# Writing out TensorE's order for the up-projections in pairs in a decoder's second MLP

## The chip, the cores and the metric

The kernel runs on one core of one Trainium2 chip, which has eight. The metric is the device time of one execution in microseconds (us), the median over several runs. One more execution was profiled; all rows of the profile are from that one.

TensorE multiplies (PE in the profile; PEld is its loading of weights, which overlaps PE), VectorE (DVE) and ScalarE (ACT) work elementwise and can read TensorE's result banks, GpSimd (POOL) works elementwise on SBUF and issues the DMAs that accumulate, SyncE (SP) issues the other DMAs.

## The reference

The reference is a decoder trunk of two layers on 512 tokens of 1024 channels, in float32: a pooling mixer in the first layer, stick-breaking attention in the second, each between RMSNorms, and each followed by an MLP with 4096 hidden channels:

```
def sq_relu_mlp(h, w_up, w_down):
    u = jnp.matmul(h, w_up)                                  # (512, 1024) x (1024, 4096)
    return jnp.matmul(jnp.square(jax.nn.relu(u)), w_down)    # (512, 4096) x (4096, 1024)
...
    x = x + rms_norm(m, mix_post_g[layer])
    h = rms_norm(x, mlp_pre_g[layer])
    x = x + rms_norm(sq_relu_mlp(h, w_up[layer], w_down[layer]), mlp_post_g[layer])
```

Only the second of these MLPs is changed.

## The kernel before

**High and low parts.** A float32 operand is written as a high part, rounded by a copy to the type float32r, and a low part, operand minus high part. A product of two operands is three matmuls: high x high, high x low, low x high. So each matmul operand costs one pass of ScalarE (the high part) and one of VectorE (the low part), in `split`, L415 and L416. In `Pair.split` (L809) the low part of some operands is made without VectorE: ScalarE writes minus the high part (L812), and a DMA issued by POOL adds the source to it (L813). `BY_DMA` names these operands.

**The MLP.** The 4096 hidden channels are 32 blocks of 128. Groups of 2, 3, 3, 3 and 3 block pairs (`GROUPS`, 28 blocks) go through `Seven`, a 2x2 scheme of seven products instead of eight for the down-projection. One of its products (L727, "down product" below) is 2 banks x n pairs x 3 matmuls of 512 columns: 18 in a group of three. `make(i)` prepares the operands of product i, two products ahead: `right` combines pieces of the down weights by VectorE (L700), `left` combines quarters of the hidden activations r, in this MLP on POOL (L681), and both are split. The down weights of the next group are loaded by SyncE while a group ends (`coming.load`). The last four blocks go through `contract` at the end (L456 to L458).

**The up-projection.** While group g is multiplied down, the hidden blocks of group g + 1 are made. In a plain block (`up`, L1050 to L1052) a weight is loaded, split (L155, L157) and multiplied by the normed input, whose parts lie in `xnh` and `xnl`: 24 matmuls of 512 columns. In the second MLP the first `PAIRED` blocks are plain, and from there on two blocks each form a `Pair`, a 2x2 scheme again: seven products of 12 matmuls with 256 columns (L865 to L867). It needs:

- combinations t1 to t4 of quarters of the input, made once (`Sums`: L780, split at L783 and L784, a list of steps, one step per down product; t4 goes into a quarter of `xnh` and `xnl` that only the plain blocks need),
- combinations of the weights, for each pair: blocks A (`raw[0]`) and B (`raw[1]`, after L839 has put a difference into half of it), and S1, S2, S4 (L838, L842, L848).

`Pair.prepare(k)` is called when product k of the pair before has been issued, because the tile that it fills is the one that product k read: 1 prepares block A, s1 and the difference; 2 block B and s2; 6 splits S2; 5 splits S1 and makes s4; 3 splits S4; 0 loads the two raw weights (L807) of the pair after. Tiles are few: two raw tiles, one `spare` tile that holds s1 and s2, one `grow` tile for s4, three `w` tiles for A and B, one tile each for the parts of S1, S2 and S4. After a product, ScalarE (L873) or VectorE (L875) takes its bank out into r; products 1, 6, 5, 3 share one half of a bank, 7 and 4 the other. Then relu and square follow on ScalarE (L877 to L885).

**What sets the order.** Each engine works through its own queue in order. The order in these queues is settled when the program is built: a planner simulates the program with estimated costs and puts next on each engine what is ready then, earlier lines of the program first. `tc.manual_schedule(engines={...})` takes engines out of the planner's hands: what they do inside the block stands in the order in which the program names it. The attention is written so for all engines, the final contraction for TensorE. The groups of the MLP are planned. The two lines that name the order of a group of pair products, three pairs a, b, c, are:

```
"a1 a2 a7 a6,a4 a5 b1 b2,a3 b7 b6,b4 b5 c1,c2 b3 c7,c6 c4 c5,c3",
"a1 a2 a7,a6 a4 a5,a3 b1 b2,b7 b6 b4 b5,b3,,",
```

The parts between commas are the pair products that the program names after down products 0 to 6; the second line is for the last group, with two pairs. `ready(g, i)` works through one part. Before the change, pairs are multiplied in groups 1 to 4 (eleven pairs, for the blocks of groups 2 to 4 and the last four), and in group 0 the seven steps of `Sums` and the preparation of pair 0 run.

Of the kernel before, what the change touches and what calls it, by code (L numbers as in the profile page):

```python
# [15 lines left out]
P = 128  # L16
# [14 lines left out]
PAIRED = 10  # L31
BY_DMA = "A B S1 S4".split()
# [61 lines left out]
def trunk(ctx, tc, x, consts, gcol, grow, pw, wup, wdn, wq, wk, wv, wo, out):  # L94
# [646 lines left out]
    class Sums:  # L741
# [3 lines left out]
        def __init__(self):  # L745
# [11 lines left out]
            self.raw, self.whole = {}, whole  # L757
# [29 lines left out]
    class Pair:  # L787
# [40 lines left out]
        def prepare(self, behind):  # L828
            on = nc.vector.tensor_tensor
            if behind == 0:  # L830
                self.load()
                return
            (a11, a12), (a21, a22) = ([x[:, c] for c in NS] for x in self.raw)
            if behind == 1:
                self.block(0)
                both = spare_tile()
                self.s1, self.s2 = both[:, NS[0]], both[:, NS[1]]
                on(out=self.s1, in0=a21, in1=a22, op=ALU.add)  # L838
                on(out=a21, in0=a11, in1=a21, op=ALU.subtract)  # L839
            elif behind == 2:  # L840
                self.block(1)
                on(out=self.s2, in0=self.s1, in1=a11, op=ALU.subtract)  # L842
            elif behind == 6:
                self.third("S2", self.s2)
            elif behind == 5:
                self.third("S1", self.s1)
                self.s4 = work.tile([P, D], F32, tag="grow", name=name("s4"))[:, NS[0]]
                on(out=self.s4, in0=a12, in1=self.s2, op=ALU.subtract)  # L848
            elif behind == 3:
                self.third("S4", self.s4)  # L850
# [40 lines left out]
    def mlp(l, mp, update):  # L891
# [53 lines left out]
        if l == 1:  # L945
# [5 lines left out]
            for g in range(1, len(GROUPS)):  # L951
                for i, cell in enumerate(FIVE[g == len(GROUPS) - 1].split(",")):
                    plan[g, i] = []
                    for w in cell.split():
                        q = 3 * (g - 1) + "abc".index(w[0])
                        plan[g, i].append((q, int(w[1])))
            plan.update({(0, n): [(-1, int(x)) for x in w] for n, w in enumerate(("", "", "", "0", "12", "65", "3"))})

        def ready(g, i):
            if g == 0:  # L960
                sums.step()
            for q, which in plan[g, i]:
# [4 lines left out]
                if which == 5 and q + 2 < len(pairs):  # L967
                    pairs[q + 2].prepare(0)
# [21 lines left out]
        for g, group in enumerate(groups):  # L990
            coming = groups[g + 1] if g + 1 < len(groups) else None
            if coming:
                coming.squares()
            ups = list(range(firsts[g + 1], firsts[g + 1] + 2 * GROUPS[g + 1]) if coming else range(plain, NJ))
            if l == 1 and g > 0:
                ups = []
            if g == 0:
                up(ups.pop(0))
            for i in range(7):
                group.product(i, y, written if g == 0 else None)  # L1000
                if 7 * g + i in steps:
                    with tc.issue_after(latest["act"].ins), tc.issue_after(latest["dve"].ins):
                        split_apart(mp)
                if l == 1 and g > 0:
                    ready(g, i)
                    fill()
                if i + 2 < 7:
                    if ups:
                        up(ups.pop(0))
                    if l == 1 and g == 0:  # L1010
                        ready(g, i)
                    group.make(i + 2)
                    if i + 2 == 4 and coming:
                        coming.load(0)
                    if i + 2 >= 5 and coming:
                        coming.load(1, NS[1] if i + 2 == 5 else NS[0])
                else:
                    if ups:
                        up(ups.pop(0))
                    if l == 1 and g == 0:  # L1020
                        ready(g, i)
                    if coming:
                        coming.make(i + 2 - 7)
                    elif i == 5:
                        piece = lambda tag, k, bufs=1: mp.tile([P, k, D], F32R, tag=tag, bufs=bufs, name=name("dn"))
                        w, e, x = piece("w1", 3), piece("e", 1), piece("w", 3, 2)
                        if l == 0:
                            both = piece("apart", 3)
                            c, d = both[:, 0], both[:, 1]
                        else:  # L1030
                            c, d = (piece(f"part{n}", 1)[:, 0] for n in ("S1", "S2"))
                            for t in range(T):
                                xt[t] = work.tile([P, D], F32, tag=f"y{t}", name=name("x"))
                                nc.sync.dma_start(xt[t], saved[t])
                        dn_pool[0] = [[w[:, 0], w[:, 1]], [w[:, 2], e[:, 0]], [c, d], [x[:, 0], x[:, 1]]]
# [674 lines left out]
```

## Time and profile before

| | |
|---|---|
| median of 3 runs | 941.97 us (939.96 to 942.34) |
| the profiled execution's own time | 941.12 us |
| its span, first to last instruction | 939.3 us |
| mean granted TensorE clock | 0.972 |
| PE busy | 891.0 us |
| DVE, ACT, POOL busy | 728.2, 590.5, 122.0 us |
| second MLP's groups 0 to 4 | 590.8 to 906 us |

A row of a group of instructions gives line, engine, operation, output and inputs, shapes and count, then the busy time, the mean of one in ns, the idle time of the engine before them and what ended it. A row of a window gives its bounds, its length, the busy time and count of PE, PEld, DVE, ACT and POOL, the granted clock, the share of the DMA engines and GB/s. Matmuls overlap: what one costs is the step from its start to the next one's start. A few matmul records are missing from the trace, so counts are taken from the code.

### The profile page before, as it was taken

How to read it: one execution, taken by the hardware profiler on the slowest of the kernel's cores; microseconds unless marked ns; L12 is line 12 of the kernel's file. 1: busy time of each engine (PE TensorE's matmuls, PEld its weight loads, DVE VectorE, ACT ScalarE, POOL GpSimd, SP SyncE). 2: the span in 40 equal slices, each digit the busy share in tenths (PEclk: the TensorE clock that was granted, in tenths of full speed). 3: DMA queues.
4: the chain of work that ended last, by engine and by line, in shares of the span. 5: the costliest groups of instructions: out<-in, count | busy, mean ns of one | idle time of the engine just before them, and what ended most of it. 6: DMA issues, size and time to landing. Idle time of an engine off the chain costs nothing.

```text
span 939.3 us, 13155 instructions
## 1 busy us (share of the span) xinstructions
PE 891.0 (95%) x5024; PEld 785.7 (84%) x5024; DVE 728.2 (78%) x791; ACT 590.5 (63%) x1014; POOL 122.0 (13%) x127
## 2 busy tenths in 40 slices
PE   9999999999999999999999999997987897898896
PEld 7998888888888888888888889886977796797786
DVE  5865998989889766669999588859866677586856
ACT  6667666577888554458957254674665755856732
POOL 2100000000000041000000010425113301502303
PEclk9999999999999999999999999997998798999999
DMA  7444466387896408755565655365556574775532
GB/s 279 171 166 166 148 235 237 135 323 277 291 340 242 183 1 282 306 216 170 183 188 184 224 186 184 110 179 140 143 154 146 115 221 101 159 222 113 154 105 89
DMA packets 54885, 175.44 MB, mean 187 GB/s; under 512 B 5488, under 2 KB 9546, under 8 KB 54822
## 3 DMA queue, kind: packets, MB, share of 16 engines
q1 hardware_dynamic: 48338, 157.28, 47.7%
q0 software_dynamic: 6336, 17.30, 9.8%
q8 instruction: 39, 0.64, 0.3%
q14 instruction: 24, 0.20, 0.1%
q10 hardware_dynamic: 148, 0.02, 0.0%
HBM read 124.64 MB, written 32.64 MB: 167 GB/s over the span
## 4 chain that ended last, share of the span: by engine, by line
PE 74%; issue 7%; DVE 7%; DMA 7%; ACT 3%; POOL 2%; POOLq 0%; DVEq 0%; SPq 0%; ACTq 0%
PE ps L727 22%; PE ps L1050 9%; PE ps L1051 9%; PE ps L1052 9%; PE ps L1334 3%; PE ps L456 2%; PE ps L458 2%; PE ps L865 2%; PE ps L457 2%; DMA raw<-in_wup 2%; PE ps L867 2%; PE ps L866 2%; PE ps L1495 2%; PE ps L1410 2%; PE ps L1189 1%
## 5 line engine op out<-in xcount | busy, mean ns | idle before, releaser
L727 PE MATMUL ps<-w,a 128*128 128x512 f32 x1176 | 275.1, 385 | 8.7 <-ACT a L415 4.7
L727 PEld LDWEIGHTS ps<-w,a 128*128 128x128 f32 x1176 | 221.6, 192 | 41.8 <-ACT a L415 6.6
L1050 PE MATMUL ps<-xnh,w 128*128 128x512 f32 (+1 forms) x528 | 186.9, 356 | 0.0
L1051 PE MATMUL ps<-xnl,w 128*128 128x512 f32 (+1 forms) x528 | 186.6, 354 | 0.1
L1052 PE MATMUL ps<-xnh,w 128*128 128x512 f32 (+1 forms) x528 | 186.6, 354 | 0.0
L1052 PEld LDWEIGHTS ps<-xnh,w 128*128 128x128 f32 x528 | 100.2, 190 | 11.0 <-DVE w L157 0.2
L1051 PEld LDWEIGHTS ps<-xnl,w 128*128 128x128 f32 x528 | 100.2, 190 | 10.8 <-DVE xnl L416 0.3
L1050 PEld LDWEIGHTS ps<-xnh,w 128*128 128x128 f32 x528 | 99.5, 190 | 11.4 <-ACT xnh L415 0.4
L415 ACT CAST w<-e 128x1536 fp32r<-128x1536 f32 (+1 forms) x30 | 41.7, 1391 | 39.7 <-DVE e L700 24.4
L416 DVE TENSOR_TENSOR a<-r,a 128x768 fp32r<-128x768 f32 (+1 forms) x60 | 54.4, 907 | 8.3 <-ACT a L415 8.2
L416 DVE TENSOR_TENSOR w<-e,w 128x1536 fp32r<-128x1536 f32 (+1 forms) x30 | 49.9, 1662 | 13.5 <-ACT w L415 13.5
L1433 DVE TENSOR_TENSOR_SCAN e<-u,begin 128x1280 f32<-128x1280 f32 x16 | 44.9, 2808 | 13.4 <-ACT u L1424 13.3
L415 ACT CAST a<-r 128x768 fp32r<-128x768 f32 (+1 forms) x60 | 47.0, 784 | 12.3 <-POOL r L681 5.7
L739 DVE TENSOR_TENSOR x<-ps,x 128x512 f32<-128x512 f32 x62 | 41.6, 685 | 13.7 <-PE ps L727 13.6
L157 DVE TENSOR_TENSOR w<-raw,w 128x1024 fp32r<-128x1024 f32 x34 | 41.5, 1220 | 13.8 <-ACT w L155 13.8
L155 ACT CAST w<-raw 128x1024 fp32r<-128x1024 f32 x34 | 35.5, 1044 | 25.1 <-PE ps L1052 24.8
L739 DVE TENSOR_TENSOR y<-ps,y 128x512 f32<-128x512 f32 x62 | 41.7, 685 | 10.5 <-PE ps L727 10.4
L415 ACT CAST w<-xn 128x1536 fp32r<-128x1536 f32 (+1 forms) x20 | 27.8, 1389 | 30.5 <-PE ps L727 30.5
L810 ACT CAST w<-raw 128x1024 fp32r<-128x1024 f32 x22 | 23.0, 1045 | 35.9 <-DMA raw<-in_wup 24.4
L486 POOL TENSOR_TENSOR y<-y,grow 128x512 f32<-128x512 f32 x4 | 6.1, 1537 | 297.5 <-ACT xn L419 297.5
L865 PE MATMUL ps<-xnh,w 128*128 128x256 f32 x132 | 38.2, 292 | 5.4 <-ACT w L810 3.0
L432 POOL TENSOR_TENSOR stat<-stat,mhalf 128x1 f32<-128x1 f32 x20 | 12.0, 599 | 218.1 <-DVE stat L423 216.8
(262 smaller groups left out, 1975.2 us busy)
## 6 DMA issues: line engine op xcount, KB each, us to landing
raw<-in_wup SPq DMA_DIRECT2D x64, 512.0 KB, 3.6
w<-kept SPq DMA_DIRECT2D x42, 512.0 KB, 5.8
w<-in_wdn SPq DMA_DIRECT2D x8, 1536.0 KB, 7.0
xn<-in_wdn SPq DMA_DIRECT2D x16, 768.0 KB, 5.6
w<-raw POOLq DMA_DIRECT2D x22, 512.0 KB, 5.3
kept<-wx SPq DMA_DIRECT2D x20, 512.0 KB, 3.8
kept<-apart SPq DMA_DIRECT2D x16, 512.0 KB, 3.9
through<-turn SPq DMA_DIRECT2D x7, 896.0 KB, 3.5
```

What stands on the lines that cost most here:

```text
L155: nc.scalar.copy(hi, raw)
L157: nc.vector.tensor_tensor(out=lo, in0=raw, in1=hi.bitcast(F32), op=ALU.subtract)
L415: latest["act"] = nc.scalar.copy(hi, src)
L416: latest["dve"] = nc.vector.tensor_tensor(out=lo, in0=src, in1=hi.bitcast(F32), op=ALU.subtract)
L727: nc.tensor.matmul(bank, a[:, x, q, TS[t]], by_twos(w[:, z, q], NS[0]), start=start and q == 0 and k == 0, stop=q == self.n - 1 and k == 2 ...
L739: nc.vector.tensor_tensor(out=part, in0=bank, in1=part, op=ALU.add)
L865: nc.tensor.matmul(bank, wh[:, ws], xs[0], start=start and k == 0, stop=False, skip_group_check=True)
L1050: nc.tensor.matmul(pu[:, cols], wh[:, k, :], xh, start=k == 0, stop=False)
L1051: nc.tensor.matmul(pu[:, cols], wh[:, k, :], xl, start=False, stop=False)
L1052: nc.tensor.matmul(pu[:, cols], wl[:, k, :], xh, start=False, stop=k == KC - 1)
L1334: nc.tensor.matmul(bank, a[x][q], in_turn(w[q // 2][z][:, cols], 512), start=(i == 0 or not linked) and q == 0 and n == 0, stop=q == 3 and ...
L1433: nc.vector.tensor_tensor_scan(out=e[:, ::-1], data0=us[a][:, 1:][:, ::-1], data1=begin[:, ::-1], initial=0.0, op0=ALU.mult, op1=ALU.max,)
```

## The change

1. `PAIRED` goes from 10 to 16: blocks 10 to 15 become plain, eight pairs remain, and they are multiplied in groups 2 to 4. Group 1 makes plain blocks. The lines of the order stay.
2. The steps of `Sums` are spread over groups 0 and 1, fourteen steps instead of seven, and pair 0 is prepared in the last three steps of group 1.
3. In groups 2 to 4 of the second MLP TensorE's order is the one in which the program names the instructions: a down product, then the pair products of its part. ScalarE, VectorE, POOL and SyncE remain planned.
4. S4 gets a tile of its own kind for all pairs, used in halves in turn, and s4 is made with s1 and s2 in `prepare(1)`. In that step s1 is named ahead of block A.
5. The low part of S1 is made by VectorE, that of S2 by DMA (before: the other way round).
6. The load of the pair after next is named after product 6 instead of 5.

```diff
-PAIRED = 10
-BY_DMA = "A B S1 S4".split()
+PAIRED = 16
+BY_DMA = "A B S2 S4".split()
...
             self.steps = [
-                [(3, "h22", "h12", minus), (3, 3, "l22", plus), (3, 3, "l12", minus)],
-                [3, (1, "h12", "h11", minus)],
-                [(1, 1, "l12", plus), (1, 1, "l11", minus)],
-                [(2, "h22", 1, minus), (2, 2, "l22", plus), 1],
-                [(4, "h21", 2, minus), (4, 4, "l21", plus), 2],
-                [4],
-                [],
+                [], [(3, "h22", "h12", minus)], [(3, 3, "l22", plus)], [(3, 3, "l12", minus)], [3],
+                [(1, "h12", "h11", minus)], [(1, 1, "l12", plus)],
+                [(1, 1, "l11", minus)], [(2, "h22", 1, minus)], [(2, 2, "l22", plus), 1], [(4, "h21", 2, minus)],
+                [(4, 4, "l21", plus), 2], [4], [],
             ]
...
             if behind == 1:
-                self.block(0)
                 both = spare_tile()
                 self.s1, self.s2 = both[:, NS[0]], both[:, NS[1]]
+                if not self.sums.fourth:
+                    self.sums.fourth.append(work.tile([P, D], F32, tag="grow", name=name("s4")))
+                self.s4 = self.sums.fourth[0][:, NS[self.j // 2 % 2]]
                 on(out=self.s1, in0=a21, in1=a22, op=ALU.add)
+                self.block(0)
                 on(out=a21, in0=a11, in1=a21, op=ALU.subtract)
+                on(out=self.s2, in0=self.s1, in1=a11, op=ALU.subtract)
+                on(out=self.s4, in0=a12, in1=self.s2, op=ALU.subtract)
             elif behind == 2:
                 self.block(1)
-                on(out=self.s2, in0=self.s1, in1=a11, op=ALU.subtract)
             elif behind == 6:
                 self.third("S2", self.s2)
             elif behind == 5:
                 self.third("S1", self.s1)
-                self.s4 = work.tile([P, D], F32, tag="grow", name=name("s4"))[:, NS[0]]
-                on(out=self.s4, in0=a12, in1=self.s2, op=ALU.subtract)
...
-            plan.update({(0, n): [(-1, int(x)) for x in w] for n, w in enumerate(("", "", "", "0", "12", "65", "3"))})
+            plan.update({(0, n): [] for n in range(7)})
+            plan.update({(1, n): [(-1, int(x)) for x in w] for n, w in enumerate(("", "", "", "0", "", "12", "653"))})
 
         def ready(g, i):
-            if g == 0:
+            if g < 2:
                 sums.step()
...
-                if which == 5 and q + 2 < len(pairs):
+                if which == 6 and q + 2 < len(pairs):
                     pairs[q + 2].prepare(0)
...
         for g, group in enumerate(groups):
+            fixed = l == 1 and g >= 2
+            with tc.manual_schedule(engines={mybir.EngineType.PE}) if fixed else nullcontext():
```

The rest of the diff indents the loop over the groups below that line and puts 2 in place of 1 where the pairs' first group is named.

More of the change, by code (lines that the diff above doesn't have):

```diff
@@ L950, in mlp @@
             pairs = [Pair(j, l, mp, sums) for j in range(PAIRED, NJ, 2)]
[L951 removed]
+            for g in range(2, len(GROUPS)):
                 for i, cell in enumerate(FIVE[g == len(GROUPS) - 1].split(",")):
@@ L990, in mlp @@
         for g, group in enumerate(groups):
[L991 to L1010, printed above, removed]
-                        ready(g, i)
[L1012 to L1035, printed above, removed]
@@ new lines, in mlp @@
+            fixed = l == 1 and g >= 2
+            with tc.manual_schedule(engines={mybir.EngineType.PE}) if fixed else nullcontext():
+                coming = groups[g + 1] if g + 1 < len(groups) else None
+                if coming:
+                    coming.squares()
+                ups = list(range(firsts[g + 1], firsts[g + 1] + 2 * GROUPS[g + 1]) if coming else range(plain, NJ))
+                if l == 1 and g > 1:
+                    ups = []
+                if g == 0:
+                    up(ups.pop(0))
+                for i in range(7):
+                    group.product(i, y, written if g == 0 else None)
+                    if 7 * g + i in steps:
+                        with tc.issue_after(latest["act"].ins), tc.issue_after(latest["dve"].ins):
+                            split_apart(mp)
+                    if l == 1 and g > 1:
+                        ready(g, i)
+                        fill()
+                    if i + 2 < 7:
+                        if ups:
+                            up(ups.pop(0))
+                        if l == 1 and g < 2:
+                            ready(g, i)
+                        group.make(i + 2)
+                        if i + 2 == 4 and coming:
+                            coming.load(0)
+                        if i + 2 >= 5 and coming:
+                            coming.load(1, NS[1] if i + 2 == 5 else NS[0])
+                    else:
+                        if ups:
+                            up(ups.pop(0))
+                        if l == 1 and g < 2:
+                            ready(g, i)
+                        if coming:
+                            coming.make(i + 2 - 7)
+                        elif i == 5:
+                            piece = lambda tag, k, bufs=1: mp.tile([P, k, D], F32R, tag=tag, bufs=bufs, name=name("dn"))
+                            w, e, x = piece("w1", 3), piece("e", 1), piece("w", 3, 2)
+                            if l == 0:
+                                both = piece("apart", 3)
+                                c, d = both[:, 0], both[:, 1]
+                            else:
+                                c, d = (piece(f"part{n}", 1)[:, 0] for n in ("S1", "S2"))
+                                for t in range(T):
+                                    xt[t] = work.tile([P, D], F32, tag=f"y{t}", name=name("x"))
+                                    nc.sync.dma_start(xt[t], saved[t])
+                            dn_pool[0] = [[w[:, 0], w[:, 1]], [w[:, 2], e[:, 0]], [c, d], [x[:, 0], x[:, 1]]]
```

4 lines of the change are left out of this document (2 added, 2 removed).

## The prediction

> **What bounds the kernel now.** I read the page's first two parts, then the windows by stage, then TensorE's waits and timeline in the second MLP, and last the chain of waits.
>
> ```profile
> span 939.3 us, 13155 instructions
> PE 891.0 (95%) x5024; PEld 785.7 (84%) x5024; DVE 728.2 (78%) x791; ACT 590.5 (63%) x1014; POOL 122.0 (13%) x127
> ...
> PEclk9999999999999999999999999997998798999999
> ```
>
> TensorE is busy 95% of the span, so it bounds the whole. But the granted clock falls only in the last third, the second MLP. The windows (time, PE, PEld, DVE, ACT, POOL busy, clock, DMA) show one group of the first MLP and then the second MLP, cut at its group borders:
>
> ```profile
> 158.00:216.00 58.00, 58.00 (x271) 50.78 (x270) 53.81 (x53) 36.45 (x43) 0.00 (x0) 1.00 0.62 225
> ...
> 590.76:647.16 56.40, 48.63 (x207) 40.17 (x206) 40.59 (x41) 33.98 (x49) 22.25 (x11) 0.92 0.50 148
> 647.16:741.00 93.84, 80.84 (x492) 75.13 (x491) 67.70 (x74) 57.87 (x89) 26.85 (x21) 0.88 0.56 137
> 741.00:809.00 68.00, 58.96 (x369) 54.13 (x368) 47.17 (x55) 42.23 (x64) 15.91 (x15) 0.92 0.61 156
> 809.00:874.00 65.00, 58.03 (x377) 53.27 (x376) 48.96 (x55) 44.88 (x68) 17.15 (x16) 0.97 0.64 163
> ...
> 906.00:930.00 24.00, 22.40 (x104) 19.10 (x104) 11.86 (x21) 5.68 (x15) 6.36 (x6) 0.93 0.11 44
> ```
>
> In the first MLP TensorE is fed without a hole while VectorE is busy 53.81 of 58.00 (93%). In the second it is neither always busy nor at full clock. What the work would cost unhindered follows from the steps of back-to-back matmuls (start, duration):
>
> ```profile
> 618.09 0.38 PE L1050 MATMUL ps<-xnh,w 128*128 128x512 f32 x1
> ...
> 623.27 0.38 PE L727 MATMUL ps<-w,a 128*128 128x512 f32 x1
> ```
> ```profile
> 663.65 0.27 PE L865 MATMUL ps<-sums,part 128*128 128x256 f32 x1
> ...
> 664.99 0.38 PE L727 MATMUL ps<-w,a 128*128 128x512 f32 x1
> ```
> ```profile
> 931.68 0.28 PE L458 MATMUL ps<-dn,sq 128*128 128x256 f32 x1
> ```
>
> Between the first two rows lie 24 matmuls of 512 columns: (623.27 - 618.09)/24 = 0.2158 us each. Between the next two lie 12 of 256 columns: 0.1117 us each. The last row ends TensorE's work at 931.8; 7.5 us of output follow.
>
> From 590.76, the first down product of the second MLP, the code issues 588 matmuls for the down products (42 per block-pair, 14 of these), 120 for five plain up blocks, 11 pairs x 84 of 256 columns, and 96 at the end: (588 + 120 + 96) x 0.2158 + 924 x 0.1117 = 173.5 + 103.2 = 276.7 us. It took 341.0. So 64.3 us are lost there, to idle time and to half clock after it. This is all there is to win.
>
> **Why it is lost.** TensorE's longest wait in total from 590 us on (us, times, longest), and the chain from 775 us (start, duration, what):
>
> ```profile
> PE ps L865 <- DVE r L875: 15.4, 7, 5.9
> ```
> ```profile
> 775.26 0.81 DMA part<-spare
> ...
> 783.42 5.79 DMA w<-raw
> ...
> 789.27 4.83 DMA raw<-in_wup
> ...
> 800.73 3.49 DMA part<-s
> 804.24 2.52 DVE s L848
> ```
>
> The planner runs down products (L727) ahead and leaves up-pair products (L865 to L867) alone at the end of each group; there each waits for the evacuation of the one before in its bank (L875), and the last pair's operands are late. The chain says why: S1's low part goes by accumulating DMA after product 5; until it lands, the single spare tile is held, so the next pair's s1 and a21 (L838, L839) wait; then B's low part by DMA, then the raw tile is free, then the next load, then A's low part, and s4 (L848) waits for the DMA of the former S4 out of the one grow tile. From 775.26 to 807 one pair costs 32 us.
>
> **The change, part by part.**
>
> *Three pairs become six plain blocks.* A pair is 84 x 0.1117 = 9.38 us, two plain blocks 48 x 0.2158 = 10.36: 3 x 0.98 = +2.9 us of TensorE. Three pairs' work on ScalarE, VectorE and POOL goes (12 accumulating DMAs); six splits of weights come; the loads are as many as before. All of it lies beside TensorE.
>
> *Group 1 is then a group like those of the first MLP*: 126 + 144 matmuls, 270 x 0.2158 = 58.3 us, against the 93.8 us that stand in the window of before (which held pairs instead). Unhindered total: 276.7 + 2.9 = 279.6; end of the span 590.76 + 279.6 + 7.5 = 877.9.
>
> *The sums of xn over two groups instead of one.* Nothing is added. VectorE's 14 passes, each 1.2 us by the row, become 6 in group 0 and 8 in group 1:
>
> ```profile
> L780 DVE TENSOR_TENSOR sum<-sum,xnl 128x1024 f32<-128x1024 f32 x3 | 3.7, 1220 | 0.0
> L157 DVE TENSOR_TENSOR w<-raw,w 128x1024 fp32r<-128x1024 f32 x6 | 7.3, 1218 | 0.0
> ```
> Group 0 lost 56.4 - 204 x 0.2158 = 12.4 us. With eight passes and pair 0's preparation gone it is bounded by 0 (first MLP) and 12.4; I take 3, near the first, as its VectorE load is now alike. Group 1's VectorE: 36 us of down operands and evacuations (rows below), 6 splits of 1.22 (second row), 8 sums, 3.5 for pair 0: 56.6 of 58.3 us, fuller than the 93% seen. Between 0 and 4; I take 2.
>
> *Order of TensorE written out in groups 2 to 4.* Pair products now follow each down product (three or four at a time; a down product is 18 x 0.2158 = 3.9 us), so an evacuation has cover except at two places per group: product 6 behind 2 and 7 (2.7 us of cover) and c5 behind c4 (1.3 us). Behind a late operand everything on TensorE queues, down products too; who feeds it must therefore keep a period of (126 x 0.2158 + 3 x 9.38) = 55.3 us. From the rows of 741 to 809 (count, busy, mean ns):
>
> ```profile
> L739 DVE TENSOR_TENSOR x<-ps,x 128x512 f32<-128x512 f32 x14 | 9.4, 686 | 6.5 <-PE ps L727 6.5
> L416 DVE TENSOR_TENSOR w<-e,w 128x1536 fp32r<-128x1536 f32 x3 | 5.3, 1753 | 0.4 <-ACT w L415 0.4
> L416 DVE TENSOR_TENSOR a<-r,a 128x768 fp32r<-128x768 f32 x5 | 4.7, 949 | 0.0
> L700 DVE TENSOR_TENSOR e<-e,w 128x1536 f32<-128x1536 f32 x1 | 1.8, 1750 | 0.0
> L838 DVE TENSOR_TENSOR spare<-raw 128x512 f32<-128x512 f32 x3 | 2.1, 689 | 4.2 <-DMA raw<-in_wup 2.7 <-ACT r L882 1.6
> L815 DVE TENSOR_TENSOR part<-spare,part 128x512 fp32r<-128x512 f32 x3 | 2.2, 717 | 0.0
> L875 DVE TENSOR_TENSOR r<-ps,r 128x256 f32<-128x256 f32 x9 | 3.8, 418 | 4.7 <-PE ps L867 4.7
> L812 ACT ACTIVATE w<-w 128x1024 fp32r<-128x1024 f32 x6 | 6.3, 1055 | 0.0
> L812 ACT ACTIVATE part<-part 128x512 fp32r<-128x512 f32 x6 | 3.7, 623 | 0.1
> L415 ACT CAST w<-e 128x1536 fp32r<-128x1536 f32 x3 | 4.4, 1467 | 2.8 <-PE ps L727 2.0 <-PE ps L867 0.8
> ```
> VectorE per group: 14 x 0.69 + 7 x 1.75 + 7 x 0.95 + 4 x 1.75 = 35.5, and per pair 4 x 0.69 + 0.72 + 3 x 0.42 = 4.7: 49.6 of 55.3 (90%). ScalarE: 14 splits, 7 of 1.47 and 7 of half the width at some 0.82, 16 us; and per pair four passes of 1024 columns, seven of 512 and seven of 256, 4 x 1.05 + 7 x 0.62 + 7 x 0.4 (the last estimated from the two widths) = 11.3: 50 of 55.3. Both fit below the 93% seen, with little to spare. Each of groups 2 and 3 is bounded by 0 and by 68 - 55.3 = 12.7 us lost; I take 4 each. Group 4 holds two pairs (45.9 us), its loss 3.
>
> *Who waits for what.* S1 by VectorE frees the spare tile a cast of 0.62 and a subtraction of 0.72 us after product 5, instead of behind a DMA; S2's DMA, which now holds it too, starts at product 6, a down product and two pair products earlier, 3.9 + 2.7 us of cover for a landing that may take 3.5 to 5.8 (the chain's part<-s and w<-raw). If that cover is short, s1 of the next pair is late by the rest, a pair before its product needs it. The count of DMAs on POOL's queue stays four per pair. S4 alternates between halves of one tile, so s4 no longer waits for the former S4 to land, and is computed at step 1: the raw tiles are no longer held until product 5, and the load two pairs ahead is issued at product 6 instead of 5. SyncE's queue then holds this load until B's DMA of the pair before has landed, with the loads of down weights behind it; they have a down product or more to spare, and cost nothing unless B lands over 4 us late. A's chain: load 4.8 + cast and negation 2.1 + DMA 5.8 = 12.7 us. It has about a pair's period (18.4 us) to run in; before it had what was left after product 5. What is late next is the first pair: its blocks need the weight tiles of plain blocks 13 and 14, and raw tiles, at the end of group 1, with some 13 us until its product 1. A loss of 0 to 6 us; I take 4.
>
> *The end.* Before, the last pair product stood in the final contraction:
>
> ```profile
> 910.19 0.48 PE L456 MATMUL ps<-dn,sq 128*128 128x512 f32 x1 [1.57 <-ACT sq L415]
> ```
> Now product b3 comes two down products earlier; 0.5 us remain.
>
> *The clock.* After idle time the granted clock is halved for a while:
>
> ```profile
> 641.00:651.00 10.00, 7.27 (x28) 6.11 (x27) 8.40 (x12) 6.67 (x8) 1.82 (x3) 0.53 0.79 211
> 730.00:740.00 10.00, 7.86 (x31) 7.20 (x32) 5.20 (x8) 7.62 (x12) 3.06 (x4) 0.52 0.55 117
> ```
> Ten microseconds at half clock cost up to 5 us of work. I allow one such stretch and a shorter one: 6 us, between 0 and the roughly 25 that clock cost before (from the clocks of the windows). The Trainium skill, "TensorE: Matmul & The Clock Gate", section "What's actually happening", has the clock drop after an idle window of about 3.4 us; by that rule gaps of 1 to 3 us would cost no clock and the sum would be 6 us lower. The trace disagrees: behind the 1.57 us gap at 910.19 the window 906 to 930 has a clock of 0.93.
>
> **Sum.** Lost: 3 + 2 + 4 + 8 + 3 + 0.5 + 6 = 26.5. Span 877.9 + 26.5 = 904.4; the profiled run stands 1.8 us above its span (941.12 against 939.3): 906.2. The median, 941.97, is 0.85 above that run, inside the runs' scatter; I predict 906.
>
> **Rivals.**
> (a) Nearly no loss, as in the first MLP: 877.9 + 1.8 + about 10 = 890. For: the 58.00 of 58.00 above. Against: ScalarE is 90% full too, and POOL lies in the operands' path.
> (b) The pairs still set the pace. For: VectorE is stretched while POOL works:
>
> ```profile
> 725.63 2.79 DVE L838 TENSOR_TENSOR spare<-raw 128x512 f32<-128x512 f32 x1 [6.08 <-DMA part<-spare]
> 725.79 2.08 POOL L681 TENSOR_TENSOR r<-r 128x768 f32<-128x768 f32 x1
> ```
> 0.69 us became 2.79. Two such per group fill VectorE to 53.8 of 55.3. At 23 us per pair, between the 18.4 that TensorE takes and the 32 of the chain, groups 2 and 3 take 69 and group 4 some 50: 13.7 + 13.7 + 4 = 31.4 lost; with 13.5 for the other terms 879.7 + 44.9 = 925. The Trainium skill, "SBUF — State Buffer", section "Who interferes with whom", has the second of the two wait fully for the shared port pair; the 2.79 us beside the 2.08 agree.
> (c) Slower than before: the accumulating DMAs sit in POOL's one queue behind combinations (L681) that wait for ScalarE's squares; with the order fixed, down products wait with them. It decides if each of 8 pairs loses 7.5 us: 880 + 60 = 940 and more, say 950. For: so long a wait of POOL ahead of such an issue exists:
>
> ```profile
> 766.24 0.89 POOL L813 DMA_DIRECT2D w<-raw  x1 [15.64 <-ACT r L873]
> ```
> Against: the planner, which still orders POOL, places the issues by when their sources are ready.
> (d) The change doesn't do what it says: operands are as late as before, and the loss of the pairs' first group, 93.8 - 55.3 = 38.5 us, moves with them into group 2; with the 12.7 of the next and 9.7 of the former third group, 879.7 + 61 = 941.
>
> **How the numbers follow.** My sum 0.56 (897 to 916); (a) 0.15; (b) 0.22; (c) 0.04; (d) 0.03. The range leaves out (c), (d), the upper part of (b) and a little of (a): 889 to 928. Faster 0.93, within 0.3% (what runs that scatter from 939.96 to 942.34 can tell) 0.03, slower 0.04.
>
> **What would show it.** Right: no up-pair products alone at the ends of groups; no wait of spare on a DMA of S1; group 1 in 58 to 61 us with TensorE full; groups 2 and 3 in 57 to 61; clock 0.97 or more in the second MLP; waits of L865 on L875 below 5 us in all. Wrong: waits of L727 or L865 on w<-raw landing, or gaps over 5 us at c1 of each group (then (b) or (c)); VectorE above 95% in groups 2 and 3; a hole before the first pair longer than 6 us.

## The result, and the profile after

| | median, µs | runs, µs | ratio to before, 95% interval |
|---|---|---|---|
| before | 941.86 | 939.96 to 942.34 | |
| changed | 925.75 | 924.26 to 926.49 | 0.9831 (0.9812 to 0.9849) |

The kernel is faster by 16 µs where 36 were forecast, inside the range and 20 µs above the predicted time. Of two kernels below (ScalarE's order written out, and the operands named behind the copy) one execution each took far longer than the others, 1867.14 and 1156.12 µs, and the times given there leave it out. The profiled run of the changed kernel took 925.98, with a span of 924.0:

```profile
span 924.0 us, 12849 instructions
...
PE 880.1 (95%) x4916; PEld 774.2 (84%) x4916; DVE 725.9 (79%) x773; ACT 575.1 (62%) x978; POOL 116.3 (13%) x115
...
PEclk9999999999999999999999999999997999999999
```

The windows cut the second MLP at its new borders: group 0, group 1, groups 2, 3 and 4, and the end with the tail of the last down product (columns as before: engines' busy times, clock, DMA).

```profile
590.72:636.70 45.98, 44.68 (x206) 38.51 (x205) 35.68 (x34) 27.57 (x40) 15.37 (x6) 1.00 0.41 146
636.70:695.00 58.30, 58.30 (x271) 51.05 (x271) 47.92 (x46) 30.91 (x36) 10.88 (x6) 1.00 0.40 120
695.00:767.00 72.00, 58.67 (x366) 53.46 (x365) 52.76 (x55) 47.80 (x69) 20.22 (x17) 0.91 0.64 164
767.00:836.00 69.00, 59.70 (x385) 54.75 (x384) 49.68 (x57) 46.34 (x69) 20.00 (x16) 0.98 0.67 164
836.00:891.70 55.70, 46.02 (x287) 41.39 (x286) 41.17 (x45) 31.20 (x48) 13.13 (x8) 0.97 0.38 113
891.70:916.20 24.50, 24.50 (x126) 21.74 (x125) 15.32 (x25) 6.04 (x15) 7.14 (x8) 1.00 0.12 48
```

Group 1 and the end are fed like the first MLP, and group 0 nearly so. Nearly everything that is lost is lost in the three groups of pairs. From 590.72 to 916.2 TensorE takes 325.5 µs for 279.6 of work: 45.9 lost. Group 0 loses 46.0 - 44.0 = 2.0, group 1 and the end nothing, so groups 2 to 4 lose 43.9. TensorE's waits from 590 to 920 (µs in all, times, longest) are 33.5 µs, three quarters of it; the rest is half clock (about 6.5, worked out in the last section) and the refilling behind each wait. The first three rows hold 30.1:

```profile
PE ps L864 <- ACT r L872: 18.5, 8, 6.6
PE ps L864 <- ACT rp L872: 7.5, 4, 4.6
PE ps L864 <- DVE r L874: 4.1, 6, 0.9
...
```

In the changed kernel L864 to L866 are the matmuls of a pair product, L872 is ScalarE's copy of products 1, 6 and 7 out of the bank, and L874 VectorE's addition of products 2, 4 and 5. So a pair product waits for the evacuation of the product before it, and the long waits are for ScalarE's copy. Why that copy is late shows in the timeline at the start of group 3 (start, duration, what; VectorE, POOL, ScalarE and TensorE in turn):

```profile
767.85 0.69 DVE L837 TENSOR_TENSOR spare<-raw 128x512 f32<-128x512 f32 x1 [2.79 <-DMA part<-spare]
...
771.46 3.38 DVE L416 TENSOR_TENSOR w<-e,w 128x1536 fp32r<-128x1536 f32 x1
...
775.37 2.76 DVE L700 TENSOR_TENSOR e<-e,w 128x1536 f32<-128x1536 f32 x1
...
771.09 2.14 POOL L681 TENSOR_TENSOR s<-r 128x768 f32<-128x768 f32 x1 [6.43 <-ACT r L884]
...
773.78 2.73 POOL L681 TENSOR_TENSOR r<-r 128x768 f32<-128x768 f32 x1
776.59 3.21 POOL L681 TENSOR_TENSOR r<-s,r 128x768 f32<-128x768 f32 x1
...
778.22 1.47 ACT L415 CAST w<-e 128x1536 fp32r<-128x1536 f32 x1 [6.69 <-DVE e L700]
779.59 0.37 ACT L872 COPY r<-ps 128x256 f32<-128x256 f32 x1
...
780.01 0.53 PE L864 MATMUL ps<-sums,w 128*128 128x256 f32 x1 [4.55 <-ACT r L872]
```

Read it backwards. TensorE has been idle for 4.55 µs behind a copy of 0.37 (product 7 of the pair, behind the copy of product 1). The copy stands in ScalarE's queue behind a cast (L415) that waits 6.69 µs for VectorE's e (L700). VectorE made e in 2.76 µs and the pass before it in 3.38, though both take 1.75 by themselves, and POOL's three combinations of the squares (L681) run beside just these passes. Ahead of them VectorE stood still for 2.79 µs: s1 of the next pair (L837) waited for S2's DMA to let go of the spare tile, and all that stood behind it in VectorE's queue waited too. At the start of group 4 the same pass waits 2.84 µs, and TensorE behind it 4.59.

### The profile page after: what moved, and what is told of

Same layout as the page of the kernel before. It is cut to its first block, busy times and chain, and to the rows that moved or that the text cites. A ratio compares the mean times of both kernels' runs of the same rounds, so it can differ in the third digit from the quotient of the medians.

```text
span 924.0 us, 12849 instructions
## 1 busy us (share of the span) xinstructions
PE 880.1 (95%) x4916; PEld 774.2 (84%) x4916; DVE 725.9 (79%) x773; ACT 575.1 (62%) x978; POOL 116.3 (13%) x115
## 4 chain that ended last, share of the span: by engine, by line
PE 77%; DVE 7%; issue 5%; DMA 5%; ACT 4%; POOL 1%; POOLq 0%; SPq 0%; DVEq 0%; ACTq 0%
PE ps L727 23%; PE ps L1052 10%; PE ps L1054 10%; PE ps L1053 10%; PE ps L1336 3%; PE ps L456 2%; PE ps L458 2%; PE ps L457 2%; PE ps L1497 2%; PE ps L864 2%; PE ps L1412 2%; PE ps L866 2%; PE ps L865 2%; PE ps L1191 2%; DMA part<-spare 1%
## 5 line engine op out<-in xcount | busy, mean ns | idle before, releaser
L727 PE MATMUL ps<-w,a 128*128 128x512 f32 x1176 | 268.5, 381 | 2.5 <-ACT a L415 1.2
L1052 PE MATMUL ps<-xnh,w 128*128 128x512 f32 (+1 forms) x576 | 205.1, 358 | 0.0
L1053 PE MATMUL ps<-xnl,w 128*128 128x512 f32 (+1 forms) x576 | 204.8, 356 | 0.1
L1054 PE MATMUL ps<-xnh,w 128*128 128x512 f32 (+1 forms) x576 | 204.8, 356 | 0.0
L1054 PEld LDWEIGHTS ps<-xnh,w 128*128 128x128 f32 x576 | 109.2, 190 | 12.2 <-DVE w L157 0.2
L1053 PEld LDWEIGHTS ps<-xnl,w 128*128 128x128 f32 x576 | 109.2, 190 | 12.1 <-DVE xnl L416 0.3
L1052 PEld LDWEIGHTS ps<-xnh,w 128*128 128x128 f32 x576 | 108.6, 190 | 12.7 <-ACT xnh L415 0.4
L415 ACT CAST w<-e 128x1536 fp32r<-128x1536 f32 (+1 forms) x30 | 41.7, 1391 | 61.7 <-DVE e L700 42.7
L155 ACT CAST w<-raw 128x1024 fp32r<-128x1024 f32 x40 | 41.8, 1044 | 40.7 <-PE ps L1054 40.3
L157 DVE TENSOR_TENSOR w<-raw,w 128x1024 fp32r<-128x1024 f32 x40 | 50.4, 1261 | 16.2 <-ACT w L155 15.9
L416 DVE TENSOR_TENSOR w<-e,w 128x1536 fp32r<-128x1536 f32 (+1 forms) x30 | 55.2, 1839 | 7.6 <-ACT w L415 7.6
L416 DVE TENSOR_TENSOR a<-r,a 128x768 fp32r<-128x768 f32 (+1 forms) x60 | 57.0, 951 | 3.2 <-ACT a L415 3.2
L415 ACT CAST a<-r 128x768 fp32r<-128x768 f32 (+1 forms) x60 | 47.1, 785 | 13.6 <-POOL r L681 9.1
L415 ACT CAST w<-xn 128x1536 fp32r<-128x1536 f32 (+1 forms) x20 | 27.8, 1389 | 25.6 <-PE ps L727 25.6
L416 DVE TENSOR_TENSOR w<-w,w 128x1536 fp32r<-128x1536 f32 (+1 forms) x20 | 32.9, 1646 | 7.1 <-ACT w L415 7.0
L416 DVE TENSOR_TENSOR w<-xn,w 128x1536 fp32r<-128x1536 f32 (+1 forms) x20 | 33.0, 1648 | 4.8 <-ACT w L415 4.6
```

Of the source, the lines that this page charges most:

```text
L155: nc.scalar.copy(hi, raw)
L157: nc.vector.tensor_tensor(out=lo, in0=raw, in1=hi.bitcast(F32), op=ALU.subtract)
L415: latest["act"] = nc.scalar.copy(hi, src)
L416: latest["dve"] = nc.vector.tensor_tensor(out=lo, in0=src, in1=hi.bitcast(F32), op=ALU.subtract)
L727: nc.tensor.matmul(bank, a[:, x, q, TS[t]], by_twos(w[:, z, q], NS[0]), start=start and q == 0 and k == 0, stop=q == self.n - 1 and k == 2 ...
L1052: nc.tensor.matmul(pu[:, cols], wh[:, k, :], xh, start=k == 0, stop=False)
```

## The experiments

Each edit is to the changed kernel unless it says otherwise; line numbers of the two-bank kernels are two higher from the pair product on. "Planned" means that TensorE's order is left to the planner in all groups. Ratios are to the kernel before, run beside each (941.7 to 944.6).

### Which part brought what

**Planned order, all else as changed.**
```diff
-            fixed = l == 1 and g >= 2
+            fixed = False
```


> The changed kernel with TensorE planned again in groups 2 to 4; all else of the change stays. From the start of group 1 to the final contraction the kernel before took 258.6 us (647.2 to 905.8) and the changed one 258.7 (636.7 to 895.4). Theory O (the written order pays, and what it gains is used up by the three more pairs' worth of plain blocks and by new waits): without it the up products pile up at the ends of groups again, 935 to 945 us. Rival G (the written order brought nothing; the gain is group 0 without the sums and the end): 920 to 928 us, the same as the changed kernel within 3 us.

916.62 µs, faster than either expectation, ratio 0.971 (0.965 to 0.9771), against 0.9831 (0.9812 to 0.9849) with the written order. The intervals don't meet: in this kernel the written order costs 9 µs by the medians, 11 by the ratios.

**The written order alone, on the kernel before** (its groups 1 to 4).
```diff
+            fixed = l == 1 and g >= 1
+            with tc.manual_schedule(engines={mybir.EngineType.PE}) if fixed else nullcontext():
```


> The kernel before with one part of the change alone: TensorE's order written out in the groups with pairs (1 to 4). Theory C (a written order lets every late evacuation hold up the down products too, 9 us in three groups as the run without it showed): no faster than before, 942 to 955 us. Rival O (the written order helps where operands of pairs are late): 925 to 938 us.

977.39, ratio 1.0379 (1.0344 to 1.0414): 36 µs slower, more than either expectation had. The first row of TensorE's waits says by what:

```profile
PE ps L865 <- ACT r L873: 33.4, 13, 5.2
```

**The later start alone, on the kernel before, planned** (`PAIRED = 16`, sums over two groups, pairs from group 2).


> The kernel before with pairs begun in group 2 and the sums spread over groups 0 and 1 alone; S1, S4, the load and the planned order as before. Theory L (the gain is group 0, 10.5 us, and the end of the last group, 5 us, and both come from beginning later): 924 to 930 us, and the shorter use of tiles gives the rest to 916.6. Rival (the tiles give nothing, all comes from beginning later): 915 to 919 us.

924.77, ratio 0.9814 (0.9788 to 0.9839).

**The tiles alone, on the kernel before, planned** (S4 in halves, s2 and s4 early, the load at product 6, S1 by VectorE and S2 by DMA).


> The kernel before with the use of tiles alone: S4 in halves, s4 and s2 made in the first step, S1's low part by VectorE and S2's by DMA, load behind product 6. Pairs begin in group 1 and the order is planned, as before. Theory T (the chain of one pair, 32 us before, loses the wait of s1 on S1's DMA and of s4 on S4's): fewer late operands at the ends of groups, 925 to 935 us. Rival (the ends of groups wait for evacuations and POOL, not for tiles): 939 to 943 us.

926.46, ratio 0.9837 (0.9796 to 0.9878).

**The same with S1 by DMA again.**
```diff
-BY_DMA = "A B S2 S4".split()
+BY_DMA = "A B S1 S4".split()
```


> The run with the use of tiles alone (926.5 us), with S1's low part by DMA and S2's by VectorE again: what remains is S4 in halves, s4 and s2 in the first step, and the load behind product 6. Theory T1 (the spare tile held by S1's DMA is the long link of the chain): most of the 15 us is lost, 934 to 942 us. Theory T4 (s4's wait for the former S4's DMA, which held the raw tiles, is the link): 925 to 930 us.

941.18, ratio 1.0001 (0.9973 to 1.0029). So all that the tiles bring is the exchange of S1 and S2; S4's halves with the early s4 and the later load bring nothing that can be measured without it. The exchange without the other three was not run.

Together, by the medians: the later start 17 µs, the exchange 15, both 25, the written order 9 back.

### What holds TensorE

**ScalarE's order written out too**, so that the copy can't be planned behind the cast.
```diff
-            with tc.manual_schedule(engines={mybir.EngineType.PE}) if fixed else nullcontext():
+            with tc.manual_schedule(engines={mybir.EngineType.PE, mybir.EngineType.Activation}) if fixed else nullcontext():
```


> ScalarE's order is written out too in groups 2 to 4, so each evacuation of a pair product stands right behind the ones before it and ahead of the splits for the down product after next. Theory H (at each group's start the evacuation of product 1 stands in ScalarE's queue behind a cast of a combination e that VectorE makes late; TensorE waits 9.1, 4.6 and 4.6 us there, with half clock behind it): these waits go, about 19 us of idle and up to 10 of half clock less some new waits of 5 to 10: 905 to 915 us. Rival (ScalarE's order is not it: whoever stands first, the work is late because VectorE and POOL are): the wait moves to L727 or to another copy, 920 to 930 us.

962.54, ratio 1.0195 (1.0141 to 1.0249): slower still. No trace shows its waits, so where it loses isn't known.

**The next operands named behind the copy of a group's product 1** (`tc.issue_after` around `make`), which takes the cast out of the copy's way.


> The changed kernel, its written order kept, with one edge in ScalarE's queue: the splits for a down product are queued behind the evacuation of a pair's product 1 where one has just been named. Theory H (TensorE waits at group starts because that evacuation stands behind a cast that waits for VectorE): the waits of 6.6, 4.6 and 4.6 us fall to about 1 each, with the half clock behind them: 908 to 916 us. Rival (the queue's order is not the cause, VectorE and POOL are late in any order): the wait moves to L727, 922 to 930 us.

925.84, ratio 0.9833 (0.9763 to 0.9902): no gain.

```profile
PE ps L864 <- ACT r L872: 14.5, 6, 7.7
PE ps L727 <- ACT a L415: 8.1, 2, 6.9
```

The copy comes earlier at some borders, and then the down product waits for the cast that was held back. Another place in ScalarE's queue does not help; the operands are late in either order.

**Two PSUM banks for a pair's products** instead of two halves of one.
```diff
-            self.bank = ps()
+            self.banks = {0: ps()}
...
+            if i == 7:
+                self.banks[1] = ps()
-            start = i in (1, 2)
+            start = i in (1, 2, 7)
```


> The two halves of a pair's result bank become two banks. Theory B (a product waits for the evacuation of the one just before it although it writes the other half, because both lie in one bank): the 16 waits of 0.5 to 1.2 us at products 5, 6 and 4, 13 us in all, mostly go, and a7 no longer waits for a1's copy (a6 does, 1.3 us later): 908 to 915 us. Theory H alone (only the queue order at group starts counts): small waits stay or move, 922 to 926. If the banks run short, TensorE waits for L739 or L874 and it is slower than 926.

918.94, ratio 0.9748 (0.9701 to 0.9794): 7 µs less than the changed kernel, between the two expectations. In the changed kernel a product waits even where it writes the half that is not being read: product 7 at each group's start for the copy of product 1, and here product 5 for the addition of product 4 (VectorE, then TensorE):

```profile
741.81 0.42 DVE L874 TENSOR_TENSOR r<-ps,r 128x256 f32<-128x256 f32 x1 [0.71 <-PE ps L866]
...
742.29 0.38 PE L864 MATMUL ps<-sums,part 128*128 128x256 f32 x1 [0.59 <-DVE r L874]
```

With two banks the short waits go, but the operands are as late as before, and now the down products stand for them:

```profile
PE ps L727 <- ACT a L415: 9.8, 2, 8.6
PE ps L866 <- ACT r L874: 7.5, 3, 7.0
...
```

**The combinations of the squares by VectorE instead of POOL.**
```diff
-            on = nc.gpsimd if self.l else nc.vector
+            on = nc.vector
```


> The combinations of the hidden activations (L681) in the second MLP go to VectorE instead of POOL: 4 more passes of about 0.85 us per group on VectorE, no elementwise work on POOL. Theory S (VectorE's passes of 0.7 to 1.75 us become 2.75 to 3.8 us while POOL combines at each group's start, and this makes the cast late): the stretched passes go, waits at group starts fall from 9.1, 4.6, 4.6 to under 2 each: 908 to 916 us. Rival (VectorE is simply full): its load grows by 3.4 us per group, 926 to 932 us.

914.98, ratio 0.9697 (0.9655 to 0.974): 11 µs less than the changed kernel, though VectorE has twenty instructions more. The passes of the down operands from 640 to 890 (count, busy, mean ns), first of the changed kernel, then of this one:

```profile
L416 DVE TENSOR_TENSOR w<-e,w 128x1536 fp32r<-128x1536 f32 x12 | 26.3, 2195 | 2.8 <-ACT w L415 2.8
L416 DVE TENSOR_TENSOR a<-r,a 128x768 fp32r<-128x768 f32 x24 | 25.4, 1062 | 0.0
L700 DVE TENSOR_TENSOR e<-e,w 128x1536 f32<-128x1536 f32 x4 | 9.0, 2252 | 0.0
```
```profile
L416 DVE TENSOR_TENSOR w<-e,w 128x1536 fp32r<-128x1536 f32 x12 | 21.0, 1751 | 1.7 <-ACT w L415 1.7
L416 DVE TENSOR_TENSOR a<-r,a 128x768 fp32r<-128x768 f32 x24 | 22.8, 949 | 0.0
L700 DVE TENSOR_TENSOR e<-e,w 128x1536 f32<-128x1536 f32 x4 | 7.0, 1748 | 0.0
...
L681 DVE TENSOR_TENSOR r<-r 128x768 f32<-128x768 f32 x7 | 6.7, 951 | 0.1
```

A combination takes 0.95 µs on VectorE and 2.1 to 3.2 on POOL. So two causes fit: POOL no longer stretches VectorE's passes, or the chain from the squares to the operand is shorter. The next kernel tests the first.

**The same, with four POOL passes beside it that nothing needs soon.**
```diff
                 sub(r11, s1, r11)
+                if self.l:
+                    for _ in range(4):
+                        nc.gpsimd.tensor_tensor(out=r22, in0=s1, in1=r22, op=ALU.subtract)
```


> The changed kernel with the three combinations of the squares in the second MLP on VectorE, as in the run that took 915.0, and four POOL passes of the same width added beside them (a difference taken four times over, which gives the same values again up to rounding), of which no path but one late operand hangs. Theory S (POOL's passes stretch VectorE's): VectorE passes of the down operands beside them are stretched again, the longest of L416 to 2.5 us or more against 1.76 without, and most of the 11 us gained by moving the combinations is lost again: 921 to 930. Rival (the gain came from a shorter chain from the squares to the operands on VectorE): the passes may be stretched but the time stays at 913 to 918.

939.59, ratio 0.9969 (0.9947 to 0.9991): 25 µs more than without the added passes, and more than was expected. In groups 1 to 4 nothing waits for what these passes make. One of the longest waits and what precedes it (TensorE, VectorE, POOL; L730 is the down product here, L681 the combination on VectorE, L688 the added passes):

```profile
863.80 1.22 PE L730 MATMUL ps<-w,a 128*128 128x512 f32 x2 [6.82 <-DVE a L416]
...
853.11 2.20 DVE L681 TENSOR_TENSOR r<-r 128x768 f32<-128x768 f32 x1
855.23 3.37 DVE L416 TENSOR_TENSOR w<-e,w 128x1536 fp32r<-128x1536 f32 x1
...
858.85 2.22 DVE L681 TENSOR_TENSOR r<-s,r 128x768 f32<-128x768 f32 x1
860.99 2.75 DVE L416 TENSOR_TENSOR a<-r,a 128x768 fp32r<-128x768 f32 x1
...
852.67 7.58 POOL L688 TENSOR_TENSOR r<-s,r 128x768 f32<-128x768 f32 x3 [3.64 <-DVE s L681]
```

The operand (L416, a<-r) comes from VectorE's combination, not from POOL's passes. The four VectorE passes take 10.5 µs; by the means of the kernel without POOL's passes they take 0.95 + 1.75 + 0.95 + 0.95 = 4.6. Those 5.9 µs are most of the 6.82 that TensorE waits. So it is shown that POOL's passes stretch VectorE's and that this costs time. Not all of the 25 µs need be that: POOL issues the accumulating DMAs from the same queue, and one of them is issued at 860.20, right behind the added passes. And how much of the 11 µs in the changed kernel is stretching, and how much the longer chain, isn't separated.

### Taken together

Four kernels combine the edits above; no new code is in them.

**Planned order, combinations by VectorE.** 

> The changed kernel with the planned order and with the combinations of hidden activations on VectorE. Each alone stood 9 and 11 us below the changed kernel (916.6 and 915.0 against 925.75). If they are separate losses (the queue that the written order blocks, and VectorE's passes stretched beside POOL): 903 to 909 us. If both took away the same waits at group starts: 913 to 917 us.

902.65, ratio 0.9589 (0.956 to 0.9617).

**Written order, combinations by VectorE, two banks.** 

> The changed kernel, its written order kept, with the combinations on VectorE and two banks per pair. If the written order costs only through products of one bank standing next to each other and through stretched passes, both are gone: 898 to 906 us, level with the planned order with combinations on VectorE (902.65). If the order itself costs (each late operand holds all that stands behind it): 908 to 915 us.

904.03, ratio 0.961 (0.9568 to 0.9652).

**Planned order, combinations by VectorE, two banks.** 

> Planned order, combinations on VectorE, two banks per pair. Left in the version with one bank are some 13 us of waits in groups 2 to 4, half of them between products of one pair. Theory B: 895 to 900 us. Rival (eight banks are too few for two pairs and two groups at once; TensorE waits for L739): 903 to 912 us.

894.38 (892.74 to 896.56), ratio 0.951 (0.9464 to 0.9556): the fastest of all. The waits from 590 to 920, first with the order written, then planned:

```profile
PE ps L727 <- ACT a L415: 6.6, 2, 4.8
PE ps L866 <- ACT r L874: 4.1, 2, 3.8
...
```
```profile
PE ps L727 <- ACT a L415: 2.7, 2, 2.0
PE ps L727 <- DVE w L416: 2.0, 1, 2.0
...
```

The written order costs 9.1 µs in the changed kernel, 12.3 with the combinations moved, 9.7 with two banks besides: about the same each time, so it is a cause of its own, beside the combinations on POOL and the banks. (904.03 alone fits the expectation that the order costs nothing once the other two are gone; but that set it beside the planned kernel with one bank, and with two banks the planned order takes 894.38.) Is it this order, or any? Three kernels with other written orders:

**Fewer pair products at the start of a group**, in the changed kernel, and the same in the kernel of 904.03.
```diff
-        "a1 a2 a7 a6,a4 a5 b1 b2,a3 b7 b6,b4 b5 c1,c2 b3 c7,c6 c4 c5,c3",
+        "a1 a2,a7 a6 a4,a5 b1 b2,a3 b7 b6 b4,b5 c1 c2,b3 c7 c6 c4,c5 c3",
```


> The changed kernel with another written order: two pair products after down product 0 instead of four, then 3, 3, 4, 3, 4 and 2. Theory W (the written order asks for the evacuations of four products of one pair at each group's start, just when VectorE, ScalarE and POOL have most to do for the down products; the planner puts down products there): the waits of 9, 4.6 and 4.6 us at group starts shrink to 2 to 3 each: 912 to 919 us. Rival (any fixed order pays for the late operands of a group's start): 922 to 932 us, with the waits moved to L727.

936.81, ratio 0.9917 (0.9887 to 0.9947): slower than the changed kernel and than either expectation.

> The same order on the run with combinations on VectorE and two banks (904.0 us written, 894.4 planned). Theory W: the two waits of 3.8 and 4.8 us at group starts go: 895 to 899 us. Rival: 902 to 908 us.

909.9, ratio 0.963 (0.9585 to 0.9676): no gain.

**More pair products at the start of groups 3 and 4**, as the planner has them in the kernel of 894.38, and the combinations and banks as there.
```diff
-        "a1 a2 a7,a6 a4 a5,a3 b1 b2,b7 b6 b4 b5,b3,,",
+        "a1 a2 a7 a6 a4 a5 b1,b2,a3 b7 b6,b4,b5,b3,",
+        "a1 a2 a7 a6 a4 a5 b1,b2 a3,b7 b6,b4 b5 c1,c2 b3 c7,c6 c4 c5,c3",
...
-                for i, cell in enumerate(FIVE[g == len(GROUPS) - 1].split(",")):
+                for i, cell in enumerate(FIVE[{2: 0, 3: 2, 4: 1}[g]].split(",")):
```


> The written order with the combinations on VectorE and two banks per pair (904.0), but in groups 3 and 4 the pair products are brought forward as the planner has them in its own order of that kernel (894.4): after the first down product of a group seven pair products instead of four. Theory W (the written order loses because too little pair work stands where the down operands of a new group are late): the waits of L727 on a at 830 and on ps at 751 in this kernel's trace go, and the time falls to 894 to 899. Rival (an order fixed ahead loses whatever it is, since the planner mixes single matmuls of both kinds by what is ready): 902 or more.

901.44, ratio 0.9556 (0.9524 to 0.9589), beside 904.03 and 0.961 (0.9568 to 0.9652): some 2.6 µs of the 9.7, with intervals that overlap, between the two expectations. The wait of 4.8 for ACT a went, and one of 6.9 came:

```profile
PE ps L727 <- DVE x L739: 7.7, 2, 6.9
...
```

Each written order left single waits of 3.8 to 7.8 µs, each behind another late operand. The planner's order differs there in more than the count of pair products: it begins the next group's first down product with a single matmul, and mixes matmuls of two products. That this is what saves the 10 µs was not shown; an order copied from it matmul by matmul was not tried.

## Why the prediction came out as it did

**The terms of the sum.** Right: the work (279.6 µs), group 1 in 58.3, group 0's loss (3 estimated, 2.0 measured), the clock (6 estimated, about 6.5 measured), no 1.57 µs hole in the contraction. Group 1 was put at 2 and lost nothing. Wrong: the idle time of groups 2 to 4, 4 + 8 + 3 = 15 estimated, 43.9 - 6.5 = 37.4 measured. The 23 µs there with the clock, less the 3.5 by which group 0, group 1 and the contraction stayed below their estimates, are about the 19.6 between the span of 904.4 and that of 924.0.

**The step that failed** is "Order of TensorE written out in groups 2 to 4". It took from the removal of lone pair products at the group ends that their waits go, and put groups 2 and 3 at a loss of 4 each; they lost 16.7 and 13.7 (72.00 and 69.00 less 55.3), the first pair and half clock included. The waits did go from the ends, but the order itself costs 9 µs in this kernel and 36 alone. The step had the reason in its own sentence, "behind a late operand everything on TensorE queues", and then judged lateness by mean load: VectorE 90% full, so fed. Measured, VectorE has room, being busy 52.76 of 72.00 µs in group 2 and 49.68 of 69.00 in group 3 (49.6 were counted), and the operand is late all the same: in the chains shown, VectorE first waits for a DMA and then makes stretched passes. A mean load does not bound the wait for one late operand.

The count of 49.6 also took VectorE's passes at their length without POOL and left the stretching to rival (b); moving the combinations off POOL wins 11 µs. With that and the planned order together the change takes 902.65, 23 µs less and a little below the 906 forecast, so these two are enough to make up the miss. The planner's order is fixed before the run too; it is not stepping aside during the run that saves it the 9 µs, and which of its differences does stays open.

**The cover of an evacuation** was counted by halves of a bank: "cover except at two places per group". The halves are not independent here: a product directly behind one of its bank has no cover, whichever half it writes. Two banks give 7 µs back.

**The first pair**, 4 estimated within 0 to 6: two waits, 2.50 and 6.58, with half clock behind them. What was named as late next, raw tiles and the weight tiles, is the first part of the chain that ends in the longer wait; the second part is stretched passes (L839, L840 and L416 take 0.68, 0.68 and 1.75 unstretched):

```profile
685.41 7.38 DMA w<-raw
...
693.28 4.44 DMA raw<-in_wup
...
699.14 1.65 DVE raw L839
700.78 2.67 DVE spare L840
703.45 3.75 DVE w L416
...
710.98 1.47 ACT w L415
...
712.78 0.58 PE ps L864
```

**Rival (b)** named 925 and the stretching, and the time is that, in part by luck. Its groups 2 and 3 at 69 are near the 72 and 69 measured. (Its 13.5 for the other terms should be 15.5 by the main sum's own terms, which makes it 927.) But its pace, VectorE filled to 53.8 of 55.3, was not the mechanism: the engine has room, and the written order, which this rival does not name, is part of the loss. Of the 43.9 µs the combinations on POOL cost 11, the written order 9 and the one bank 7 in runs that change one of them alone; all three edits together win 31.4 (925.75 to 894.38), so they add up to a little more than their sum of 27. Rival (a)'s 890 is nearly reached by that kernel.

**The change's other parts.** S1 by VectorE was the right reading: with S2 by DMA it is worth 15 µs beside the other edits of tiles. S2's DMA holds the spare tile in its place, and VectorE waits for it about as long in all as before (6.8 µs, 7.7 before), in shorter pieces. The prediction gave this DMA 3.9 + 2.7 µs of cover and took a short cover to cost nothing, s1 being ready a pair before its product needs it. The cover was short: at the end of group 2 the DMA is issued 2.7 µs behind product 6 and takes 6.63 to land. And it is not s1's product that waits but VectorE's queue, in which the down product's e stands behind s1. In the planned kernel (916.62) VectorE does not wait for this DMA at all. What these waits cost was not tested alone. Of "what would show it": group 1 and the ends of groups came right; groups 2 and 3 took 72 and 69 µs instead of 57 to 61, the clock was 0.91 to 0.98 there, and one wait in the first pair was longer than 6 µs, as the text had for the wrong case. Waits on w<-raw landing and a VectorE above 95% did not come, and L865's waits on L875 (now L864 on L874) are 5.3 in all, close to the 5 named.

## What to carry to other kernels

An order written out by hand takes from the planner the means of putting other work ahead of an operand that it expects late: before fixing it, look for the latest operand at each border, not for the mean load of who makes it, and run the same kernel with the order left to the planner. Work given to POOL because it is idle is not free where VectorE feeds the engine that bounds: price the VectorE passes that run beside it. Test each part of a change by itself; here one part had the opposite sign, and the best kernel (894.38) keeps the other two, drops it, and adds the moved combinations and the second bank.

## What the runs showed of the hardware

**VectorE beside POOL.** Passes of 1.75 µs took up to 3.83, of 0.95 up to 2.59, of 0.68 up to 2.75, and POOL's own of 2.06 up to 3.25. VectorE's busy time does not rise when POOL's combinations are moved onto it, 725.9 µs for 773 instructions in the changed kernel, 725.1 for 793 in that of 914.98:

```profile
PE 877.6 (96%) x4916; PEld 772.2 (85%) x4916; DVE 725.1 (80%) x793; ACT 574.6 (63%) x978; POOL 65.1 (7%) x95
```

The Trainium skill, "SBUF — State Buffer", section "Who interferes with whom", has the second wait fully for the shared port pair. In the changed kernel VectorE's pass at 771.46, 1.75 by itself, begins 0.37 behind POOL's of 2.14 and takes 3.38, its own time and nearly all that was left of POOL's, which agrees. The prediction's pair agrees in length (0.69 + 2.08 for 2.79), though there VectorE's row begins first.

**A bank's halves.** A matmul into one half waited for the reading of the other half, 0.6 to 0.9 µs behind VectorE's addition and 0.5 to 1.2 behind ScalarE's copy where that was not late. Whether the chip asks for this or the program's own semaphores do isn't shown.

**The clock.** A wait of 2.50 µs was enough to halve it. The matmuls begin at full speed and slow 1.1 µs later (start, duration):

```profile
704.08 0.38 PE L864 MATMUL ps<-sums,w 128*128 128x256 f32 x1 [2.50 <-ACT r L872]
...
704.86 0.28 PE L864 MATMUL ps<-sums,w 128*128 128x256 f32 x1
...
705.14 0.42 PE L866 MATMUL ps<-sums,w 128*128 128x256 f32 x1
```
```profile
705.00:718.70 13.70, 7.12 (x27) 6.19 (x26) 12.66 (x10) 6.84 (x10) 5.59 (x4) 0.50 0.46 124
780.00:783.50 3.50, 3.03 (x13) 2.73 (x13) 3.50 (x4) 3.16 (x5) 0.50 (x1) 0.51 0.00 0
848.40:851.80 3.40, 2.85 (x12) 2.13 (x10) 3.40 (x4) 3.40 (x7) 0.88 (x1) 0.50 0.00 0
```

It stays at 0.50 for 3.4 µs behind a single wait of 4.59, and for 13.7, four times as long, where the second wait of 6.58 falls into the first stretch. Length alone does not decide: in the kernel of 914.98 waits of 1.72 and 1.87 (before 772.52 and 840.29) left the clock at 1.00, where the prediction has 0.93 behind one of 1.57. The Trainium skill, "TensorE: Matmul & The Clock Gate", section "What's actually happening", has the drop after an idle window of about 3.4 µs; the wait of 2.50 doesn't agree, and it was right to keep a term for the clock. Its 6 µs was near: in the three windows TensorE is busy 7.12 + 3.03 + 2.85 = 13.0 µs at half clock, and half of that, about 6.5 by this estimate, is lost.
